# A table that sets the order of the engines' queues ahead of the FFN

## The chip, the cores and the metric

The kernel runs on one core of one Trainium2 chip. The metric is the device time of one execution in microseconds (us). A core has a matrix engine (PE, TensorE), a vector engine (DVE), a scalar engine for activations (ACT), a small general engine (POOL) and a queue that issues transfers (SP). Each of them works through its own queue of instructions in the order of that queue, and waits at an instruction until what it needs from the others is there. PE writes its results to PSUM, eight banks of 512 floats per partition; ACT and DVE read them from there.

## The reference

The reference is one block of a decoder, on 512 tokens of width 1024, all in float32:

```python
h = rmsnorm(x, norm1_g) * (1.0 + scale1) + shift1        # scale, shift, gate: c_act @ w_ada + b_ada
proj = h @ w_in                                          # x_rnn 1280, q_lat 384, kv_lat 256, k_rope 32, g_rnn, g_mla 1024 each
xc = causal_dwconv(x_rnn, conv_w, conv_b)                # width 4
y_rnn = rg_lru(xc, positions, ...)                       # two gates, a = exp(..), h[t] = a[t] * h[t-1] + b[t]
q = rmsnorm(q_lat) @ w_uq; kv = rmsnorm(kv_lat) @ w_ukv  # 16 heads, rotary on 32 of 96 columns
y_mla = causal_block_attention(q, k, v)
merged = sigmoid(g_rnn) * (y_rnn @ w_proj_rnn) + sigmoid(g_mla) * (y_mla @ w_proj_mla)
x = x + gate1 * (merged @ w_out)
h2 = rmsnorm(x, norm2_g) * (1.0 + scale2) + shift2
u = causal_dwconv(h2 @ w_up, ffn_conv_w, ffn_conv_b)     # 2 x 2816 columns, width 3
x = x + gate2 * ((silu(u_gate) * u_val) @ w_down)
return rmsnorm(x, final_g)
```

## The kernel before

**Tiles.** Columns of the weights lie on 128 partitions, the 512 tokens on the free axis, so one matmul is 128 x 128 weights by 512 tokens. For precision every operand is kept in two parts, a high one and the rest: `split` (L132, L133) copies the high part on ACT and subtracts it on DVE. A product then takes three matmuls (`mm3`, L164 to L166): high by high, high by low, low by high. Weights come by SP into one of three load buffers, `raw` (512 KB each), and are split from there into tiles `whl` and `whg`, two of each; one such tile is a *unit* of 512 columns, four blocks of 128, which twelve matmuls use. `Stream.get` (L153 issues its load) does this for the weights of all projections.

**PSUM.** The eight banks are shared out by tag: three `tr`, one `fil`, one `gm`, three `acc`. A new user of a bank waits until ACT or DVE has read the old one's result.

**Stages.** (1) *Start*: the modulation vectors of the first norm (DVE), the norm itself, transposes and the product with the latent columns. (2) *Attention*: 16 heads. `head_a` makes the scores, their maxima on DVE and the exponentials on ACT (L643), and transposes the result; `head_b` multiplies by the values. Between them stand the products for the next group of heads (`q_nope`, `k_nope`, `v_group`, all in bank `fil`) and 32 *fills*: halves of the products for the two merging gates, mostly in bank `gm`. Each second fill ends with a tanh that empties the bank (L466 ACT). `sums_rows` turns the sums of the softmax (L817) and spreads their inverses over the partitions with eight loads on POOL's queue (the spread loads, L823); `y_split` multiplies by them (L828). (3) *Recurrence*: `rnn_tile` for ten tiles of 128 channels: a product (bank `tr`), the convolution on DVE (L784), two gates (bank `acc`), tanh and exp on ACT (L792 to L797), a square root (L801), a scan on DVE (L805) and a last split into `yr`. Products of the attention's output, `pm_tile` 0 to 7, fill PE between the tiles. (4) *Projections*: eight products of the recurrence's result (called projection 0 to 7 here), each over ten chunks, chunk k being tile k; then the output product `wo` and, for each of four token blocks, the residual (L880, L881), the square (L913), the second norm (L915), transposes (L920), scale and shift (L925, L927) and a split (L929, L930). (5) *FFN*: 44 products with convolution, gating, and 22 chunks of the last product.

**What sets the order.** The code writes the operations in the order of its loops. A planner then puts each engine's instructions in a queue of their own: it goes through the program with estimated durations and takes, of what could run, what has the highest priority. The code steers it with `tc.high_priority(offset=...)`, with constants like `AHR` or `LOW` as offsets, and with `tc.issue_after(...)`, which fixes that one instruction stands behind another. PE's queue of before therefore mixes products where two had the same rank: the matmuls of fills 0 and 2 alternate one by one, and so do those of projections 2 and 3. Which buffer of a tag a tile gets also follows from that order.

Of the kernel before, what the change touches and what calls it, by code (L numbers as in the profile page):

```python
# [91 lines left out]

@with_exitstack
def block_kernel(ctx, tc, a):
    nc = tc.nc
# [670 lines left out]
    def tok(t):  # L766
        return slice(t * P, (t + 1) * P)

    with phase("p_rnn") as p2:
# [40 lines left out]
        def sums_rows():  # L810

            V.reciprocal(sums, sums)
            b = bank("tr")
# [3 lines left out]
            S.activation(rt[:HEADS, :], b[:HEADS, :], AF.Copy)  # L817
# [83 lines left out]
        h2 = st(sb, "A", 1, [P, NK, 2, T], F32R)  # L901
        for t in range(4):
            b = bank("fil" if t % 2 else "gm")
            for k in range(NK):
# [8 lines left out]
            S.activation(f[:, :T], x1[t][:, T:], AF.Square, accum_out=ssq)  # L913
# [1 line left out]
            V.tensor_scalar(f, x1[t], r[:, 0:1], -0.5, MUL, MUL)  # L915
            for i in range(2):
                b = bank("tr", (P, 4, P))
                for q in range(4):
                    k = 4 * i + q
                    PE.transpose(b[:, q, :], f[:, k * P:(k + 1) * P], ident)  # L920
# [8 lines left out]
                S.activation(dh, hi, AF.Copy)  # L929
# [208 lines left out]
```

## Time and profile before

| | |
|---|---|
| median of three runs | 888.75 us (887.96 to 891.56) |
| the profiled execution | 887.65 us |
| its span, from the first to the last instruction | 885.8 us |
| PE, matmuls | 859.3 us busy, 4030 instructions |
| PE, loading weights (runs beside the matmuls) | 688.8 us, 4030 |
| DVE | 643.3 us, 1212 |
| ACT | 491.1 us, 898 |
| POOL | 18.7 us, 43 |
| HBM read | 103.59 MB |

The profile gives, for each instruction, its line, the tile that it writes and those that it reads, its start and its duration, and what ended the idle time of its engine before it. `tr<-A,whl` is a product of activations `A` with weights `whl` into a bank of tag `tr`. A table of stretches gives, for each stretch of time, the busy time of each engine in it, the number of instructions in brackets, the clock granted to PE as a share of full speed, and the mean share of time in which the sixteen DMA engines were busy.

### The profile page before, as it was taken

Reading aid. Unit: us, or ns where it says so; the run is one execution under the profiler, and the core shown is the slowest. Engines: PE = TensorE matmul, PEld = TensorE weight load, DVE = VectorE, ACT = ScalarE, POOL = GpSimd, SP = SyncE. Lnnn points to the kernel's source line nnn. Section 1 sums busy time; section 2 is a strip of 40 time slices with the busy share of each in tenths; the row PEclk is TensorE's granted clock in tenths of the full one; section 3 lists DMA queues with packets and bytes.
Section 4 is the critical chain, followed back from the end, with each engine's and each line's share of the span. In section 5 each row is a group of like instructions: output and inputs, shape, how many; then the busy total and the mean of one; then the engine's idle time right before and its main releaser. Section 6 shows DMA issues by size and latency. Waiting matters only on the chain.

```text
span 885.8 us, 11220 instructions
## 1 busy us (share of the span) xinstructions
PE 859.3 (97%) x4030; PEld 688.8 (78%) x4030; DVE 643.3 (73%) x1212; ACT 491.1 (55%) x898; POOL 18.7 (2%) x43
## 2 busy tenths in 40 slices
PE   7999999999999999999999999999999999999996
PEld 4777878788767777777878898888788888888885
DVE  7978887989866899998555879766666666423524
ACT  7575777667645888887333554444544444322323
POOL 0001000001020000000000000000000000000000
PEclk9999999999999999999999999999999999999999
DMA  9824233344462243354325074332233333333322
GB/s 347 342 66 113 73 99 116 78 143 138 143 168 95 101 160 120 122 195 156 100 76 161 22 261 142 100 95 95 85 93 93 92 94 92 95 96 95 96 72 95
DMA packets 33804, 109.08 MB, mean 123 GB/s; under 512 B 4290, under 2 KB 8002, under 8 KB 33748
## 3 DMA queue, kind: packets, MB, share of 16 engines
q1 hardware_dynamic: 32116, 103.60, 35.7%
q0 software_dynamic: 1632, 4.75, 2.3%
q8 instruction: 32, 0.52, 0.2%
q14 instruction: 24, 0.20, 0.1%
HBM read 103.59 MB, written 2.13 MB: 119 GB/s over the span
## 4 chain that ended last, share of the span: by engine, by line
PE 63%; ACT 3%; DVE 3%; DMA 2%; issue 1%; POOL 0%; ACTq 0%; POOLq 0%; DVEq 0%
PE acc L164 9%; PE acc L166 9%; PE acc L165 9%; PE tr L164 4%; PE tr L166 4%; PE tr L165 4%; PE acc L762 2%; PE acc L764 2%; PE acc L763 2%; PE tr L1004 2%; PE tr L1006 2%; PE tr L1005 2%; PE gm L164 1%; PE gm L166 1%; PE gm L165 1%; PE fil L762 1%
## 5 line engine op out<-in xcount | busy, mean ns | idle before, releaser
L133 DVE TENSOR_TENSOR whg<-raw,whg 128x512 fp32r<-128x512 f32 x119 | 81.5, 688 | 82.1 <-ACT whg L132 81.8
L132 ACT ACTIVATE whl<-raw 128x512 fp32r<-128x512 f32 (+2 forms) x131 | 74.9, 577 | 112.4 <-PE acc L166 26.5
L132 ACT ACTIVATE whg<-raw 128x512 fp32r<-128x512 f32 x119 | 74.2, 627 | 103.3 <-PE acc L166 53.9
L133 DVE TENSOR_TENSOR whl<-raw,whl 128x512 fp32r<-128x512 f32 (+2 forms) x131 | 80.8, 622 | 52.9 <-ACT whl L132 52.3
L166 PE MATMUL acc<-A,whg 128*128 128x512 f32 x176 | 70.1, 398 | 0.1
L164 PE MATMUL acc<-A,whg 128*128 128x512 f32 x176 | 69.9, 397 | 0.3 <-ACT whg L132 0.2
L165 PE MATMUL acc<-A,whg 128*128 128x512 f32 x176 | 69.5, 395 | 0.0
L958 DVE SCALAR_TENSOR_TENSOR Y<-acc,vec,Y 128x511 f32<-128x511 f32 x86 | 64.3, 748 | 1.3
L166 PE MATMUL acc<-A,whl 128*128 128x512 f32 x160 | 63.2, 395 | 0.0
L165 PE MATMUL acc<-A,whl 128*128 128x512 f32 x160 | 63.2, 395 | 0.0
L164 PE MATMUL acc<-A,whl 128*128 128x512 f32 x160 | 63.1, 395 | 0.0
L643 ACT ACTIVATE P<-P,mx,qsc 128x512 f32<-128x512 f32 (+1 forms) x64 | 41.2, 647 | 7.1 <-DVE mx L639 7.0
L164 PEld LDWEIGHTS acc<-A,whg 128*128 128x128 f32 x176 | 33.0, 187 | 9.4 <-ACT whg L132 1.4
L166 PEld LDWEIGHTS acc<-A,whg 128*128 128x128 f32 x176 | 33.0, 187 | 8.9 <-DVE whg L133 0.7
L165 PEld LDWEIGHTS acc<-A,whg 128*128 128x128 f32 x176 | 33.0, 188 | 7.6
L164 PE MATMUL gm<-A,whg 128*128 128x512 f32 x88 | 35.7, 405 | 1.7 <-ACT R L466 1.2
L165 PEld LDWEIGHTS acc<-A,whl 128*128 128x128 f32 x160 | 30.0, 188 | 7.3
L956 ACT ACTIVATE Y<-acc,vec 128x512 f32<-128x512 f32 x43 | 32.9, 764 | 5.1 <-PE acc L166 5.1
L166 PEld LDWEIGHTS acc<-A,whl 128*128 128x128 f32 x160 | 30.0, 188 | 7.1
L164 PEld LDWEIGHTS acc<-A,whl 128*128 128x128 f32 x160 | 30.0, 188 | 7.1
L166 PE MATMUL gm<-A,whg 128*128 128x512 f32 x88 | 35.4, 403 | 0.0
L165 PE MATMUL gm<-A,whg 128*128 128x512 f32 x88 | 35.0, 398 | 0.0
(509 smaller groups left out, 2276.1 us busy)
## 6 DMA issues: line engine op xcount, KB each, us to landing
raw<-in_w_up SPq DMA_DIRECT2D x44, 512.0 KB, 3.5
raw<-in_w_dn SPq DMA_DIRECT2D x22, 512.0 KB, 3.6
wa<-in_w_adat SPq DMA_DIRECT2D x16, 512.0 KB, 9.7
raw<-in_w_adat SPq DMA_DIRECT2D x16, 512.0 KB, 3.3
raw<-in_w_xr SPq DMA_DIRECT2D x10, 512.0 KB, 4.1
raw<-in_w_pr SPq DMA_DIRECT2D x10, 512.0 KB, 3.8
raw<-in_w_gm SPq DMA_DIRECT2D x8, 512.0 KB, 3.6
raw<-in_w_gr SPq DMA_DIRECT2D x8, 512.0 KB, 3.5
```

Of the source, the lines that this page charges most:

```text
L132: S.activation(h, src, AF.Copy)
L133: return V.tensor_tensor(dst[:, 1, lo_c:lo_c + n], src, h.bitcast(F32), SUB).ins
L164: PE.matmul(out, wh, x[:, 0, xs], start=start, stop=False)
L165: PE.matmul(out, wh, x[:, 1, xs], start=False, stop=False)
L166: return PE.matmul(out, wl, x[:, 0, xs], start=False, stop=stop).ins
L643: S.activation(pq, pq, AF.Exp, scale=qsc[:, qb:qb + 1], bias=mx[:, qb:qb + 1], accum_out=sm[:, qb:qb + 1])
L762: PE.matmul(out, lt[:, 0, s], w[:, 0, :], start=start, stop=False)
L763: PE.matmul(out, lt[:, 0, s], w[:, 1, :], start=False, stop=False)
L764: return PE.matmul(out, lt[:, 1, s], w[:, 0, :], start=False, stop=stop).ins
L956: S.activation(u, b, AF.Identity, scale=vc("fw", 2 * 2 * NF + cj), bias=vc("fb", cj))
L958: V.scalar_tensor_tensor(u[:, d:], b[:, :T - d], vc("fw", (2 - d) * 2 * NF + cj), u[:, d:], MUL, ADD)
L1004: PE.matmul(b, lt[:, 0, s], w[:, 0, o:o + n], start=start, stop=False)
```

## The change

A table, `QUEUES`, holds one row for each of the five queues. `queue_order()` runs once, right before the FFN's code. It collects the instructions written so far, engine by engine, in the order in which the code wrote them, numbers them from 0 in base 36, and reads the engine's row: `9` is one entry, `b-c` a run of entries. Between each two neighbours of the row it adds a dependency of the kind NoSync, an order within one queue without a semaphore. The planner still runs; up to the FFN it has no choice of order left within a queue. No operation, tile or load is added or taken away. In ACT's row the first 25 entries, which hold the first norm's, are in the order that they had before.

The diff, with the table cut to the rows that are spoken of:

```diff
+QUEUES = {
+    "PE": """
+        0-8 b-c 9 d a e-u w-x 1h-1i v 10 13 y 1j 16 19 1c z 1k 11 14 12 15 22-25 17-18 1a-1b 1d-1g 1l 1o 1m 2n-2q 1n
...
+        r2-r3 wa wd wj-wk we-wi wb-wc wl vs-vz ry-s9 ty-u9 w0-w5 wm-wn w6 wo-wp v4 wq-wt w7-w9 v5-v7 wu-wv v8-v9
...
+        111 11e-11p zk-zp 11w-11x zq-zs 11y-127 zt-zz 128-129 100-103 11q 11t 12a-12c 11u 11r-11s 11v 12d-12j
+        12q-12t 13e-13f 12u-12v 13g-13p 12w-12z 13q-13r 130-136 13s-141 12k-12p 137-13d 148-14h 14w-14x 14i-14n
...
+        1bw-1bx 1cg-1cp 1by-1c1 1cq-1cr 1c2-1c5 1cs-1d1 1c6-1cd 1bk-1bm 1d8-1d9 1bn-1bp 1da-1dh 1d2 1d5 1di-1dl 1d6
+        1d3-1d4 1d7 1dw 1dm-1dv 1dx-1ej 1eq-1et 1fk-1fl 1eu 1fm-1fv 1ek-1ep 1ev-1ez 1fw-1fx 1f0 1ge-1gf 1fy-1gd
+        1gg-1ip 1f1 1iq 1f2 1ir 1f3 1is 1f4 1it 1f5 1iu 1f6 1iv 1f7-1fj 1iw-1jq 1kk-1kl 1jr-1kb 1kx 1kc-1kd 1ky
...
+    "DVE": """
+        0-3 a 4 b 5-9 c-k o l-m p-q n u-w s r t 10-12 y x z 16 14 17-18 13 15 1c-1d 1a 1e 19 1b 1i 1g 1j 1f 1h 1o 1u
...
+        ak-al an-ao c9 cb ap ca cc-cd cf aq ce cg-ch ar cj ci cl cn ck as cm co bu at bv c0 bw cp bx au by-bz cq c2
...
+        jz jt jy k0-k5 kc-kd k7-ka k6 kb ke-ki kp-kq kk-kn kr-kv kj ko kx-l0 kw l1""",
+    "Activation": """
+        0-3 6-7 4 8 5 9-n p o q s r t v-w u x-y 11 z-10 12 17-18 13-15 1g-1p 1w 16 1u 1q 1v 1r 1a 1y 8h-8i 19 1b
...
+        77 72 6w 73 7a 78 7b 7i-7k 7n-7q 7c 6n 7r-7s 7l 7v 7m 7w-7y 7d 7t 83 7z-80 7u 81 8j 82 85 84 86 88 8x-8y 87
+        89 8z-90 8b 91-92 8a 8c 93-94 8k-8l 8e 8o 8m 95 8d 8f 8n 96 8p 99 8q-8r 8t 8s 9i 97 8u-8v 9j 98 8w 9v-9w 8g
...
+        c6-c7 c9 cv c8 ck-cl cw cm-co cy ca cz cp cb d1 cq cc cr d2-d3 cx d5-d6 d8-da dc-dd df-dh dj d0 d4 dk d7 db
+        de dm-do di dq-dr dl ds-dt dp du-dv e2-e3 dw-dx e4-e9 dy-e1 ea-en eq eo-ep er-es ey et ez eu-ex f0-f5""",
+    "Pool": """
+        0 2 1 3-g i h j m l k n 11 p-q o r-10""",
+    "SP": """
+        0 2-a c b d-t 1 u-z 1b 10-1a 1c-25 2p 26-2o 2q-3g 3p-3q 3h-3k 3r-3s 3l-3o 3t-41""",
+}
...
+    def queue_order():
+        queues = {}
+        for ins in nc.cur_bb.bb.instructions:
+            if type(ins).__name__ not in ("BassTilePoolBoundary", "InstRegisterMove"):
+                queues.setdefault(str(ins.engine).split(".")[-1], []).append(ins)
+        for name, table in QUEUES.items():
+            order = []
+            for run in table.split():
+                ends = [int(v, 36) for v in run.split("-")]
+                order += queues[name][ends[0]:ends[-1] + 1]
+            for before, after in zip(order, order[1:]):
+                tc.add_manual_dep(after, before.name, mybir.DependencyInfo(
+                    mybir.DependencyClass.NoSync, mybir.DependencyReason.DATA), reason="order")
+
+    queue_order()
```

Some entries, to follow the table by: on PE, fill 21 is ty to u9 and fill 22 is v4 to vf; projection 0 is 1dw to 1ep (its last chunk 1en to 1ep), projection 1 is 1eq to 1fj, projection 5 is 1i2 to 1iv. On DVE, au splits the weights of fill 31, he is the last split of tile 9, kp and kq are L880 and L881 of the last token block. On ACT, 7d is the tanh of fill 21, 8f copies the weights of fill 31, ca and cp are the square roots of tiles 8 and 9, ey is the square (L913) of the last token block.

More of the change, by code (lines that the diff above doesn't have):

```diff
@@ L90 @@
 EARLY = 4
+QUEUES = {
+    "PE": """
+        0-8 b-c 9 d a e-u w-x 1h-1i v 10 13 y 1j 16 19 1c z 1k 11 14 12 15 22-25 17-18 1a-1b 1d-1g 1l 1o 1m 2n-2q 1n
+        1p-21 26-27 29 38-3b 28 2a-2m 2r 3t-3w 2s-37 3c-3s 3x 40 43 46 49 3y-3z 41-42 44-45 47-48 4a-4b 4e-4g 4c-4d
+        4h-4w 5j-5k 4x-5i 5l 7s-7t 5m-5r 7j-7q 7u-80 5s-66 7r 67-68 81-82 69-6v 83-89 6w-78 8m-8r 79-7c 91 94 9a 7d
+        92-93 9b 95-99 9c ba 8s-90 bb-bd bj-bk be-bi bl 7e-7h 9d-9h 9l 9i-9k 9m 7i 9n-9y 8a-8h 9z-ab bm-bp ac-ae
+        bq-bt 8i af-ao bu bw-bz cp cs cy bv 8j-8l c0 ct-cx c1-c3 cq-cr ap-ax cz-d0 ea ed-ei eb-ec ay-b1 ej-el b2
+        c4-cc b3-b9 dj-do cd-cl d1-d5 d9 d6-d8 da cm-co dy dp-dr db-dc em-et dd-di ds-dt eu-ev du-dx fg fj fp-fq
+        fk-fo fh-fi fr ew dz ex hp-hr e0 g2-gd hs-hx ey e1 ez e2 f0 e3 f1 e4 f2 e5 fs-fz f3 e6 ge-gp g0 gq-gt g1
+        e7-e9 gy-h3 gu-gx hy-hz j4 j7 i0 f4 j8-jc j5-j6 f5 jd-jf h4-hc f6-f7 i1-i5 i9 i6-i8 ia f8-fd ib-id ij-ir
+        jg-jj ie-ii fe-ff jk-jn kp ks ky-kz kt jo-jp ku-kx kq-kr l0 jq jy-jz jr-ju k0 hd k1 he k2 hf k3 hg-hi jv-jx
+        hj-hm lj-ll hn-ho lm-lt k4-k5 ng-ni k6-kc l1 l5-l9 l2-l4 la nj-nr lb-lf lu m5-mg lg-li is-ix mh-ms iy-j1 lv
+        lz m3 m0-m2 lw-ly n1-n6 m4 j2-j3 kd mt-mx p7-pa my-n0 pb-pf ke-kf n7-nf ns-nw o0 nx-nz o1 kg-km o2-o6 kn pg
+        ko o7-o9 ph-pi r4 r7-rc r5-r6 oa-oi rd-rf oj-om q1-q6 pj pn-pr pk-pm ps on-ow pt ox pu-px q7-qa py-q0 qb-qf
+        oy-p6 rg-rn sa sd-si sb-sc sj-sk sw ro-rp sl ua-ui rq-rx sx-t7 uj-ul qg-qj sm sq-st sn-sp t8-tb su-sv tc-tj
+        qk-qt tk-tm ts-tu tn-to tv-tx tp-tr um uq-ut vg vj vp un-up vh-vi vk-vo uu-uv vq-vr qu-qv uw-v0 qw-r1 v1-v3
+        r2-r3 wa wd wj-wk we-wi wb-wc wl vs-vz ry-s9 ty-u9 w0-w5 wm-wn w6 wo-wp v4 wq-wt w7-w9 v5-v7 wu-wv v8-v9
+        ww-wx 104-107 wy-x3 va-vf x4-z4 108-109 z5-z8 10a-10v z9-zf 112-113 zg-zh 114-11d zi 10w 10z zj 110 10x-10y
+        111 11e-11p zk-zp 11w-11x zq-zs 11y-127 zt-zz 128-129 100-103 11q 11t 12a-12c 11u 11r-11s 11v 12d-12j
+        12q-12t 13e-13f 12u-12v 13g-13p 12w-12z 13q-13r 130-136 13s-141 12k-12p 137-13d 148-14h 14w-14x 14i-14n
+        14y-157 142-147 158-159 14o-14s 15a-15j 14t-14v 15q-15v 16e-16f 15w-15x 16g-16p 15y-163 16q-16r 164-165
+        16s-16z 15k 170-171 15n 166-167 15l-15m 15o-15p 168-16d 178-17v 172 175 17w 173-174 176-177 17x-18h 18q-18r
+        18i-18j 18s-18y 19e-19f 18z-190 19g-19p 18k 18n 191-193 18l-18m 18o-18p 194 19q-19r 195 19s-1a1 196-19d
+        1a8-1a9 1aw-1ax 1aa-1aj 1ay-1b7 1ak-1an 1a2 1a5 1b8-1b9 1ao 1a3-1a4 1a6 1ba-1bj 1a7 1ap-1av 1bq-1bv 1ce-1cf
+        1bw-1bx 1cg-1cp 1by-1c1 1cq-1cr 1c2-1c5 1cs-1d1 1c6-1cd 1bk-1bm 1d8-1d9 1bn-1bp 1da-1dh 1d2 1d5 1di-1dl 1d6
+        1d3-1d4 1d7 1dw 1dm-1dv 1dx-1ej 1eq-1et 1fk-1fl 1eu 1fm-1fv 1ek-1ep 1ev-1ez 1fw-1fx 1f0 1ge-1gf 1fy-1gd
+        1gg-1ip 1f1 1iq 1f2 1ir 1f3 1is 1f4 1it 1f5 1iu 1f6 1iv 1f7-1fj 1iw-1jq 1kk-1kl 1jr-1kb 1kx 1kc-1kd 1ky
+        1ke-1kg 1ko 1kh 1kp 1ki 1kq 1kj 1l0-1l2 1kr 1ku-1kw 1l6-1l8 1ks-1kt 1kz 1l9-1la 1l3-1l4 1li 1lc 1l5 1lb
+        1ll-1lm 1lj-1lk 1lu-1lw 1ld-1le 1km-1kn 1lo-1lq 1lf-1lh 1ln 1lx-1ly 1m6-1m8 1mi-1mk 1m0 1mu 1m1-1m2 1lr
+        1mv-1mw 1ls-1lt 1lz 1m9-1ma 1mc-1md 1n6 1me 1m3 1n7-1n8 1m4-1m5 1mb 1ml-1mm 1mo-1mq 1mf-1mh 1mn 1mx-1my
+        1n0-1n2 1mr-1mt 1mz 1n9-1na 1n3-1n5 1nb 1o8-1oc 1nc-1nz 1od-1ou 1o0-1o7 1ov 1p4-1pr 1q0-1q2 1ow-1p3 1q3-1qn
+        1ps 1pw-1py 1pt-1pv 1pz 1qo-1qv""",
+    "DVE": """
+        0-3 a 4 b 5-9 c-k o l-m p-q n u-w s r t 10-12 y x z 16 14 17-18 13 15 1c-1d 1a 1e 19 1b 1i 1g 1j 1f 1h 1o 1u
+        1p 1v-1w 1k 1q 1x 1l 1y bs br 1z 1m 20 1s 21 1r 22 1t 1n 23 27-28 24-26 2d-2e 2g 2f 2i 2h 33-35 39 36-37
+        2j-2m 38 2n-2p 29 2v-2y 3a-3c 2a 2z 31 3d 30 32 3e 2b 3f 2q av ax 2r aw 2s ay 2t-2u az-b1 2c b2-b5 3g 3j
+        b6-b8 3h b9-bb 3i 3m bc-bf 3k 3x bg-bh 3p 3l bi 3q-3s bj 3t bk-bq 49 3n 4a-4c 3o 3y 3u 4d 3v 48 3w 3z 42 40
+        45 4e-4f 4p 41 43 4i 4g 44 4o 4r 4h 4s-4t 4q 46 4u 50 47 4v 58-5c 4j-4k 53 4l 57 56 4m 51 4n 52 4w-4y 5h 5q
+        5d-5e 4z 5f 54 5r 5j 5i 55 5k-5l 63 5m 64-65 5s 5n-5o 5g 5v 5t 5y 5p 61 5w 5u 66 5x 67 6k-6n 6c 6o 62 5z 68
+        60 69-6a 6j 6t 6d-6f 6b 6g 6q 6p 6h-6i 71-74 6r 6w 6u 75 70 6s 6v 7b-7d 6z 7a 7j 6x 7v 76-77 6y 7k 78 7e
+        7w-7y 7f 7l 79 7z 7u 7m 7o 7r 7g-7h 7p 7i 8f 7q 8a 8g-8h 84 7n 8c 7s 80-81 7t 8d 82 8e 8o 8i 8b 83 8j 8x-8z
+        85-87 90 88 8r 8w 8p 8l 8k 8q 8u 8m 89 91 97 8s-8t 8v 92 99 98 9a 93-94 9b 9g 9c 9h 8n 9r-9u 9i 9v 95 9p 9l
+        9d 9j 9e 96 9f 9q 9m 9k a4 9n 9w-9x a5-a7 9y a8 a1 ae-af 9o ad ag a9-aa ah a2 9z-a0 a3 bt ab am ai-aj ac
+        ak-al an-ao c9 cb ap ca cc-cd cf aq ce cg-ch ar cj ci cl cn ck as cm co bu at bv c0 bw cp bx au by-bz cq c2
+        cv c1 dj c3 d4 c4 cr dk c5 cs c6 ct c7 d5 cu c8 dl-dm da cx do d6 cw d7 e3 cy d8 cz dp e4 d0 d9 d1-d2 dq du
+        d3 e5 dr dn dc e6 db e8 ds dd dt de en-eo df e9 dg dw ee dv dh ep e7 eq es di dx ea dy eb f7 et f8 ec dz-e0
+        ed e1 eu ey f9 e2 er ev eg fa fc ef ew eh ex ei fr-fs ej fb ek fd el fi ez em ft-fu f0 fe fw ff-fg f1 gb fh
+        gc f2 fx f3-f4 g2 fk f5 fj gd f6 fv ge fy gg fl fz fm g0 fn gv g1 gh fo gw fp g4 fq gi gm gx gf gy h0 gj g3
+        gk g5 gl g6 h1 hf g7 hg g8-g9 h2 h6 h3 gz hh h4 ga go hk h5 gn hi hl gp h8 h7 hm hj gq h9 hq ha gr hr hb gs
+        hv hc gt hd gu he hn-ho hw-hx hp i1 hy-hz i2 i6 i3 i7-i8 ic i9-ia id ih ie ii if ij hs in ht i4 hu i0 io i5
+        ib ig is ik-il it im iu-iv ip-ir iw-iz je-jf j0-j1 jg-jk j2 j8 j3 j9 jb j4-j5 jc j6 jl j7 ja jd jm-js ju-jx
+        jz jt jy k0-k5 kc-kd k7-ka k6 kb ke-ki kp-kq kk-kn kr-kv kj ko kx-l0 kw l1""",
+    "Activation": """
+        0-3 6-7 4 8 5 9-n p o q s r t v-w u x-y 11 z-10 12 17-18 13-15 1g-1p 1w 16 1u 1q 1v 1r 1a 1y 8h-8i 19 1b
+        1s-1t 1x 1d 1c 1e 1z 22 20-21 25 23 2f 24 28-29 26 2a-2b 27 2g 2c-2d 1f 2q 2e 2h 2s-2v 2k 2i 2n 2w-2x 33 2j
+        2l 30 2y 2m 32 2z 2o 3c 2p 34-36 3k 3f 3l-3m 2r 3i 3n 3d 37 31 3e 38-39 3s 3a 40 3o-3p 3b 3q 3g 41 3h 3t-3w
+        42 3x-3y 3r 45 43 48 3z 3j 4b 46 44 47 4l 4d-4g 49 4o 4h 4a 4i-4j 4p 4w 4q-4s 4k 4n 4t 4z 4u 4m 4x 4v 4y
+        54-55 4c 52 56-57 5j 50 58-59 51 5a 5k-5l 5b-5f 5m 5o 5r 5u 5g-5h 5p 5i 5v-5w 5q 64 5x 62 5n 5s 5y-60 5t 6f
+        53 65 61 67-6a 6i 6g 63 6b-6d 6h 6l 6o-6p 6j 6q-6r 6k 6m 6s-6t 74 66 6e 6u 75 6x-6z 76 70 6v 7e-7g 79 7h 71
+        77 72 6w 73 7a 78 7b 7i-7k 7n-7q 7c 6n 7r-7s 7l 7v 7m 7w-7y 7d 7t 83 7z-80 7u 81 8j 82 85 84 86 88 8x-8y 87
+        89 8z-90 8b 91-92 8a 8c 93-94 8k-8l 8e 8o 8m 95 8d 8f 8n 96 8p 99 8q-8r 8t 8s 9i 97 8u-8v 9j 98 8w 9v-9w 8g
+        9m 9a 9x 9k 9b-9c 9e 9d 9y 9f 9l 9g 9z a1 9h aa 9n ab-ac 9o-9p 9r 9q a0 9s ad a2 ag a3 9t a4 ap a5 aq-ar 9u
+        a6 ae a7 as af a8 at av b4 a9 ah b5-b6 ai-aj al ak au am aw b7 an ba ax ao bj-bk b8 bl ay-b0 b9 b1 bm bb bp
+        b2 bc by bn b3 c0 bz bd-bg bo c1 bh bq bi c2 c4 cd br ce-cf bs bu bt c3 cg bv-bw ch cj bx cs-ct c5 cu ci
+        c6-c7 c9 cv c8 ck-cl cw cm-co cy ca cz cp cb d1 cq cc cr d2-d3 cx d5-d6 d8-da dc-dd df-dh dj d0 d4 dk d7 db
[5 more added lines that the diff above has]
+}
```

## The prediction

> **What bounds the kernel now.** I read the page's head first, then one table of stretches cut where the kernel's stages change, then the waits of TensorE (PE), then the timeline at the places where a wait ends. The head gives the whole:
>
> ```profile
> span 885.8 us, 11220 instructions
> ...
> PE 859.3 (97%) x4030; PEld 688.8 (78%) x4030; DVE 643.3 (73%) x1212; ACT 491.1 (55%) x898; POOL 18.7 (2%) x43
> ```
>
> PE is busy 97% of the span: 885.8 - 859.3 = 26.5 us idle. The table of stretches (length, then busy time and instructions of PE, weight loads PEld, DVE, ACT, POOL; clock; DMA share; GB/s) says where:
>
> ```profile
> 0.00:52.00 52.00, 46.96 (x182) 32.02 (x182) 44.19 (x98) 32.55 (x50) 1.70 (x12) 0.97 0.79 304
> 52.00:246.00 194.00, 187.65 (x1008) 153.66 (x1009) 166.31 (x421) 137.48 (x316) 10.88 (x21) 1.00 0.36 110
> 246.00:270.00 24.00, 22.34 (x97) 16.68 (x96) 15.26 (x25) 11.86 (x22) 5.20 (x9) 1.00 0.63 160
> 270.00:290.00 20.00, 19.24 (x83) 14.66 (x82) 12.13 (x20) 11.01 (x18) 0.00 (x0) 1.00 0.23 79
> 290.00:416.00 126.00, 122.65 (x516) 94.25 (x515) 116.73 (x180) 106.18 (x158) 0.00 (x0) 1.00 0.43 146
> 416.00:500.00 84.00, 83.45 (x367) 66.73 (x367) 51.44 (x92) 32.12 (x64) 0.00 (x0) 1.00 0.30 94
> 500.00:520.00 20.00, 18.48 (x135) 16.89 (x134) 16.45 (x38) 14.01 (x32) 0.95 (x1) 1.00 0.50 153
> 600.00:700.00 100.00, 100.00 (x431) 80.35 (x430) 69.06 (x100) 46.13 (x74) 0.00 (x0) 1.00 0.31 95
> 800.00:886.00 86.00, 78.57 (x404) 66.44 (x402) 35.97 (x72) 26.28 (x52) 0.00 (x0) 0.97 0.26 86
> ```
>
> Two blocks of idle are out of the table's reach or nearly: 52 - 46.96 = 5.0 us at the start, and 86 - 78.57 = 7.4 us at the end, behind the FFN. What a new order can touch is 6.35 (52 to 246, attention) + 1.66 + 0.76 + 3.35 (290 to 416, the recurrence) + 0.55 + 1.52 = 14.2 us.
>
> That is idle time alone. In the FFN (600 to 700) PE runs 431 matmuls in 100 us, 0.232 us each, with no idle: this is its full pace. At that pace the 516 matmuls from 290 to 416 would take 119.7 us, so 6.3 us are lost there where only 3.35 show as idle. The rest is the slow restart around each wait, which the records hide because one of them is longer (0.47 us in the row quoted further down) than its share of the pace. I take lost time as 1.9 times idle (6.3 / 3.35).
>
> **Which waits.** The waits of PE that lie past the start (what waited, for whom: us in total, times, longest):
>
> ```profile
> PE gm L164 <- ACT R L466: 1.9, 2, 1.2
> PE fil L611 <- DVE q L575: 1.6, 2, 1.3
> PE tr L164 <- ACT whl L132: 1.4, 3, 0.8
> PE tr L166 <- DVE whl L133: 1.0, 1, 1.0
> ...
> PE gm L166 <- DVE whg L133: 0.9, 1, 0.9
> ...
> PE tr L920 <- DVE R L915: 0.7, 1, 0.7
> ...
> PE acc L164 <- ACT A L929: 0.7, 1, 0.7
> ```
>
> None of these is a lack of work on ACT (55% busy) or DVE (73%). Each is an instruction that stood in its engine's queue behind another one, or a PSUM bank that PE wanted again at once.
>
> **The change part by part.** No operation is added, removed or resized: 2264 matmuls, 758 DVE, 546 ACT, 38 POOL and 145 SP instructions of the part up to the FFN get a fixed place. An entry is the instruction's number, in base 36, on its engine in the order in which the code writes them. The table's last SP run ends at 41 (number 145), one past the queue's last, 40, and a slice that ends too far takes nothing more. I followed the numbers through the code and set the table against the order in the trace.
>
> *Loads (SP, POOL).* Both rows are the order of before but for some swaps of neighbours. Cost 0; what moves is when their buffers come free.
>
> *Start, 0 to 52.* ACT's first 25 entries are as before. On DVE the two copies of the broadcast conditioning (a, b) now stand among the first norm's small operations instead of behind them. ACT, which reads that result, is still occupied with its squares then, and with DMA at 0.79 share the stretch waits for its loads. I take 0, between -0.5 and +0.5 us.
>
> *Attention and fills, 52 to 270.* Here is the largest wait, with what ACT did meanwhile:
>
> ```profile
> 247.59 0.59 ACT L817 ACTIVATE yr<-tr 16x512 f32<-16x512 f32 x1
> 248.09 0.57 ACT L466 ACTIVATE R<-gm 128x512 f32<-128x512 f32 x1
> ```
>
> ```profile
> 247.03 0.47 PE L166 MATMUL gm<-A,whg 128*128 128x512 f32 x1
> 248.71 0.51 PE L164 MATMUL gm<-A,whg 128*128 128x512 f32 x1 [1.21 <-ACT R L466]
> ```
>
> One bank serves the fills: fill 22 may start only when the tanh of fill 21 has read it, and that tanh (entry 7d) stood behind a copy for the softmax sums. PE lost 248.71 - 247.03 - 0.23 = 1.45 us. In the table 7d stands ahead of 7t, so ahead of these copies, and eleven other matmuls (w0-w5 wm-wn w6 wo-wp, about 1.3 us by their columns at the full pace) stand between the last of fill 21 (u9) and the first of fill 22 (v4). The same is done for the second such wait (1.9 - 1.2 = 0.7 us): sixteen matmuls, 16 x 0.232 = 3.7 us, now part the bank's old user from its new one. These two waits should go; what hides them is PE's own other work. At y_split, whose multiplications wait for the spread loads, one more weight split (ao) stands ahead of the waiting DVE instruction.
>
> The other attention waits I can't follow one by one. Some distances shrink: between the scores of head 5 and its transposes 4.8 us of matmuls (by columns at the full pace) stand where 8.6 stood, so new waits will come. All lost time here is 1.9 x (6.35 + 1.66) = 15.2 us, the most that can be won. The other bound is a loss of 2 us, if the waits move and the tight places add one like that at 247 and a half. I take 7, a little under half: DVE is busy 166.31 of 194 us here, so there is slack to use, but 86% leaves queues that jam.
>
> *Recurrence, 270 to 416.* This stage is bound by DVE more than by PE: 116.73 of 126 us. Two edits bear on it. First, the last fill's weight split (au on DVE, 8f on ACT) comes about 16 places earlier; it frees a load buffer, for which these stood waiting:
>
> ```profile
> 282.47 0.33 SPq L153 DMA_DIRECT2D raw<-in_w_xr  x1
> ...
> 286.79 0.63 ACT L132 ACTIVATE whl<-raw 128x512 fp32r<-128x512 f32 x1 [0.83 <-DMA raw<-in_w_xr]
> ...
> 287.48 0.50 PE L164 MATMUL tr<-A,whl 128*128 128x512 f32 x1 [0.76 <-ACT whl L132]
> ```
>
> Second, tiles 8 and 9 share one square-root stretch on ACT: ck-cl, cm-co (tile 9's tanh and exp) come ahead of ca, cp (both square roots). Each switch of function set costs a load:
>
> ```profile
> L801 ACT ACT_TABLE_LOAD x10 | 12.8, 1283 | 0.2
> L792 ACT ACT_TABLE_LOAD x8 | 10.3, 1283 | 0.1
> ```
>
> Two of these go, 2.6 us of ACT next to the end of the chain. DVE's idle time is 7.87 (270 to 290) + 9.27 (290 to 416) = 17.1 us; more than that the chain of ten tiles can't be shortened, and part of it is the chain's own latency. I take 7, between 0 and 14.
>
> *The price.* Tile 9's result gates the rest:
>
> ```profile
> 415.18 0.69 DVE L133 TENSOR_TENSOR yr<-pr,yr 128x512 fp32r<-128x512 f32 x1
> ...
> 416.01 0.43 PE L165 MATMUL tr<-yr,whl 128*128 128x512 f32 x1
> ```
>
> The matmul at 416.01 (1eo, projection 0, last chunk) starts when DVE has split tile 9. Before, 1864 PE instructions of this part stood ahead of it; in the table 1841 do, mostly because 19 matmuls of projection 1 (1f1 to 1fj), which filled this place, are put behind projection 4. PE will thus ask for tile 9 after 23 matmuls fewer: 23 x 0.232 = 5.3 us. PE's remaining work behind the gate is longer by as much. So the gate must open 5.3 us sooner only to break even: +5.3, a fixed term.
>
> *Projections to the second norm, 416 to 520.* Projection 1's late matmuls hold one whg and one whl weight tile, so projections 2 to 5 stream through one tile of each kind instead of two. A unit of weights is 12 matmuls, 2.8 us, and its two halves take about 0.6 us (ACT) and 0.7 us (DVE), with DVE busy 51.44 of 84 us: cover enough, I take +0.3, and up to 5 if half a microsecond is lost on each of ten units. At the end, the last token block waited for this:
>
> ```profile
> 504.47 0.69 DVE L880 TENSOR_TENSOR T<-fil,acc 128x512 f32<-128x512 f32 x1
> ...
> 511.17 0.69 DVE L881 TENSOR_TENSOR T<-T,Y 128x512 f32<-128x512 f32 x1
> ...
> 511.89 0.63 ACT L913 ACTIVATE R<-T 128x512 f32<-128x512 f32 x1 [0.48 <-DVE T L881]
> ```
>
> Between L880 and L881 lay 6 us of other DVE work. The table puts L881 (kq) right behind L880 (kp), and ACT's ey ahead of et; the two PE waits on L915 and L929 (0.7 each, 1.4) should go. I take -1.3, between 0 and 1.9 x 1.52 = 2.9.
>
> **Sum.** 0 - 7 - 7 + 5.3 + 0.3 - 1.3 = -9.7 us against the profiled execution, whose own time is 887.65 (span 885.8 and 1.85 around it): 878.0. The median of the runs is 888.75, 1.1 above it, so 879.
>
> [...]
>
> **The rivals.** *Waits only move (886.7).* For it: DVE at 86% in attention and 93% in the recurrence, in-order queues, and tighter places in the table. Against: the places I could follow are each cleared by what stood in the way. Half the gain of each stage: -3.5 - 3.5 + 5.3 + 0.3 - 0.7 = -2.1 from 887.65, then + 1.1, gives 886.7.
>
> *Slower: the gate at tile 9 (894).* Place: 1eo. If the chain of ten tiles, paced by DVE and by its loads, ends at 415.9 as now, everything PE won before stands still in front of it, and 5.3 us more work lie behind: 888.75 + 5.3 = 894. It decides where DVE's last split of tile 9 comes less than about 1 us earlier; from 1 to 5.3 us it is a draw. Against it: the chain starts only when attention is over, so what is won there moves its start too.
>
> *Far faster (869).* PE restarts cost as much as the idle time, so clearing a wait pays twice: 15.2 x 0.8 in attention, 12 of DVE's idle in the recurrence, 2.5 at the end: -12.2 - 12 + 5.3 - 2.5 = -21.4, 867 to 869. Against it: it needs 93%-busy DVE to become nearly gapless.
>
> **How the numbers follow.** The forecast, 879, has its own range 873 to 885 and a chance of 0.51. Waits only move: 0.21. Gate: 0.13. Far faster: 0.15. A measurement of this kernel can tell about 0.5%, 4.4 us, from no change: faster is under 884.3, slower over 893.2. Faster: 0.51 less 0.03 of its upper edge, 0.15, and 0.02 of the second case: 0.65. Slower: the gate, 0.13. The rest, 0.22. The range reaches from 867.5 to 891: the gate and a little below are left out, under 0.2.
>
> **What would show it.** Right: no PE wait on L466; the 1.28 us table loads number 25 instead of 27; the last split of tile 9 near 402 and projection 0's last chunk just behind it; PE idle from 52 to 270 near 4; no 0.7 us waits on L915 and L929. Wrong: PE idle for microseconds just ahead of projection 0's last matmuls (the gate); new waits on the weight splits of projections 2 to 5; waits in attention as long in sum as now under other names.

## The result, and the profile after

The changed kernel takes 878.94 us (878.41 to 880.0, four runs) against 888.45 (887.96 to 891.56) of the kernel before: a ratio of 0.9887, 95% interval 0.9863 to 0.9912, 9.5 us less. Forecast were 879.0, and 9.7 less. The profiled execution took 880.0, that of before 887.65; the sections below say why these two differ by 7.65 only. One execution of rec (2971.41 us) and the profiled one of gateloads (2919.74) took over three times as long as all others; the ratios leave them out, and the two medians hold them and would be 0.13 us or less lower without.

The head of the page of the changed kernel, and its table of stretches (columns as before). The table in the kernel adds 72 lines, so L466 is now L538, L132 and L133 are L204 and L205, L915 is L987; lines behind `queue_order()` stand 94 later (L1006 is L1100). In most kernels of the experiments lines stand one or two lower, by the length of their tables.

```profile
span 878.2 us, 11212 instructions
...
PE 858.8 (98%) x4030; PEld 688.6 (78%) x4030; DVE 640.6 (73%) x1212; ACT 488.1 (56%) x896; POOL 18.7 (2%) x43
```

```profile
0.00:52.00 52.00, 46.80 (x178) 32.27 (x179) 44.52 (x100) 32.70 (x50) 1.70 (x12) 0.93 0.77 296
52.00:246.00 194.00, 191.44 (x1038) 157.23 (x1037) 166.42 (x421) 140.39 (x319) 11.33 (x22) 1.00 0.36 116
246.00:270.00 24.00, 22.99 (x95) 17.14 (x94) 15.83 (x26) 11.53 (x21) 4.70 (x8) 1.00 0.65 174
290.00:416.00 126.00, 124.48 (x519) 94.57 (x518) 117.43 (x184) 102.56 (x156) 0.00 (x0) 1.00 0.44 145
500.00:520.00 20.00, 20.00 (x173) 20.00 (x172) 18.32 (x37) 11.77 (x25) 0.17 (x1) 1.00 0.82 282
```

PE's idle time from 52 to 270 us fell from 8.0 us to 2.56 + 1.01 = 3.6, from 290 to 416 from 3.35 to 1.52, from 500 to 520 from 1.52 to nothing. Over the whole span it fell from 26.5 to 878.2 - 858.8 = 19.4 us: 7.1 of the 7.6 us by which the span is shorter are idle time of PE that is gone. Its waits past the start that are 0.3 us or longer in sum are now these:

```profile
PE tr L236 <- ACT whl L204: 1.3, 2, 1.0
PE acc L703 <- DMA q<-rp: 0.8, 1, 0.8
PE tr L725 <- DVE Y L743: 0.7, 1, 0.7
PE tr L238 <- DVE whl L205: 0.6, 1, 0.6
PE tr L237 <- DVE yr L205: 0.5, 1, 0.5
PE fil L236 <- DVE spc L823: 0.4, 1, 0.4
PE tr L992 <- DVE R L987: 0.3, 1, 0.3
PE gm L834 <- DVE T L952: 0.3, 1, 0.3
```

No wait on the tanh (L538) is left, and that was the largest sum of before past the start, 1.9 us. The tanh of fill 21 (7d) runs as soon as its bank is full:

```profile
238.69 0.60 ACT L538 ACTIVATE R<-gm 128x512 f32<-128x512 f32 x1 [0.16 <-PE gm L238]
```

**Where the time went.** I cut both traces at places that are the same work: the last matmul of the latent columns, the last split of the attention's output (ysplit), tile 9's last split, the last product of the first half of `wo`, and PE's last matmul. Before (tile 9's row, 415.18, stands in the prediction), then after:

```profile
51.29 0.63 PE L406 MATMUL tr<-A,wls 128*64 128x512 f32 x2
268.20 1.29 DVE L133 TENSOR_TENSOR yhl<-Y,yhl 128x512 fp32r<-128x512 f32 x2
479.87 0.39 PE L764 MATMUL gm<-whg,yhl 128*128 128x512 f32 x1
878.29 0.28 PE L1006 MATMUL acc<-A,ff 128*128 128x256 f32 x1
```

```profile
52.63 0.62 PE L478 MATMUL tr<-A,wls 128*64 128x512 f32 x2
264.24 1.28 DVE L205 TENSOR_TENSOR yhl<-Y,yhl 128x512 fp32r<-128x512 f32 x2
403.84 0.69 DVE L205 TENSOR_TENSOR yr<-pr,yr 128x512 fp32r<-128x512 f32 x1
473.10 0.39 PE L836 MATMUL gm<-whg,yhl 128*128 128x512 f32 x1
870.16 0.28 PE L1100 MATMUL acc<-A,ff 128*128 128x256 f32 x1
```

From the ends of these rows, and of the same rows in the traces of the experiments (us; the last column leaves the start out):

| kernel | latents end | attention: to ysplit | chain: ysplit to tile 9 | tile 9 to `wo` half | to PE's end | sum behind the latents |
|---|---|---|---|---|---|---|
| before | 51.9 | 217.6 | 146.4 | 64.4 | 398.3 | 826.6 |
| after | 53.3 | 212.3 | 139.0 | 69.0 | 396.9 | 817.2 |
| att | 52.3 | 211.2 | 148.1 | 64.4 | 397.8 | 821.5 |
| rec | 52.3 | 217.1 | 140.9 | 69.0 | 396.5 | 823.5 |
| stall | 51.6 | 214.0 | 139.3 | 69.0 | 396.5 | 818.9 |
| start | 53.1 | 212.6 | 139.4 | 69.0 | 396.6 | 817.7 |
| fill31 | 52.3 | 211.5 | 145.2 | 69.0 | 396.5 | 822.2 |
| loads2 | 53.6 | 211.9 | 142.9 | 69.3 | 396.6 | 820.7 |
| pair | 51.7 | 211.9 | 142.9 | 69.0 | 396.5 | 820.3 |
| gate | 51.9 | 211.7 | 139.2 | 70.9 | 396.5 | 818.3 |
| gate5 | 52.1 | 212.2 | 139.9 | 69.1 | 396.5 | 817.7 |
| gateloads2 | 53.1 | 212.2 | 142.0 | 73.9 | 396.6 | 824.7 |
| tail | 52.1 | 211.5 | 140.2 | 69.0 | 396.5 | 817.2 |

Attention -5.3, chain -7.4, behind the chain +4.6, output and FFN -1.4: -9.5 in all. Against the -9.5 stands +1.3 at the start of this one execution. Chain and what follows it have to be read together, -2.8: PE is busy nearly all the time, so work that it no longer does ahead of tile 9 it does behind it. Eight of the traces have the changed kernel's order up to ysplit, and their second column goes from 211.5 to 212.3 (att, 211.2, nearly so); in the last column after and tail agree, at 817.2, and start lies 0.5 above. So differences under 0.8 us in the one and 0.5 in the other say nothing.

### The profile page after: what moved, and what is told of

Same layout as the page of the kernel before. It is cut to its first block, busy times and chain, and to the rows that moved or that the text cites. A ratio compares the mean times of both kernels' runs of the same rounds, so it can differ in the third digit from the quotient of the medians.

```text
span 878.2 us, 11212 instructions
## 1 busy us (share of the span) xinstructions
PE 858.8 (98%) x4030; PEld 688.6 (78%) x4030; DVE 640.6 (73%) x1212; ACT 488.1 (56%) x896; POOL 18.7 (2%) x43
## 4 chain that ended last, share of the span: by engine, by line
PE 72%; DVE 10%; ACT 8%; DMA 7%; issue 3%; POOL 0%; SPq 0%; DVEq 0%; ACTq 0%; POOLq 0%
PE acc L237 9%; PE acc L238 9%; PE acc L236 9%; PE tr L238 3%; PE tr L236 3%; PE tr L237 3%; PE acc L834 2%; PE acc L836 2%; PE acc L835 2%; DMA wa<-in_w_adat 2%; PE tr L738 2%; PE tr L1098 2%; PE tr L1100 2%; PE tr L1099 2%; PE gm L236 2%
## 5 line engine op out<-in xcount | busy, mean ns | idle before, releaser
L205 DVE TENSOR_TENSOR whg<-raw,whg 128x512 fp32r<-128x512 f32 x119 | 81.6, 688 | 86.8 <-ACT whg L204 86.5
L204 ACT ACTIVATE whl<-raw 128x512 fp32r<-128x512 f32 (+2 forms) x131 | 75.2, 576 | 110.8 <-PE acc L238 29.5
L204 ACT ACTIVATE whg<-raw 128x512 fp32r<-128x512 f32 x119 | 74.2, 627 | 98.5 <-PE acc L238 58.6
L205 DVE TENSOR_TENSOR whl<-raw,whl 128x512 fp32r<-128x512 f32 (+2 forms) x131 | 81.3, 621 | 56.2 <-ACT whl L204 55.9
L1052 DVE SCALAR_TENSOR_TENSOR Y<-acc,vec,Y 128x511 f32<-128x511 f32 x86 | 64.4, 749 | 1.3
L715 ACT ACTIVATE P<-P,mx,qsc 128x512 f32<-128x512 f32 (+3 forms) x64 | 41.2, 645 | 17.5 <-DVE mx L711 17.5
```

The source lines that it names most:

```text
L204: S.activation(h, src, AF.Copy)
L205: return V.tensor_tensor(dst[:, 1, lo_c:lo_c + n], src, h.bitcast(F32), SUB).ins
L715: S.activation(pq, pq, AF.Exp, scale=qsc[:, qb:qb + 1], bias=mx[:, qb:qb + 1], accum_out=sm[:, qb:qb + 1])
L1052: V.scalar_tensor_tensor(u[:, d:], b[:, :T - d], vc("fw", (2 - d) * 2 * NF + cj), u[:, d:], MUL, ADD)
```

## The experiments

**Two halves.** *att* takes the changed kernel's order for what starts ahead of 266 us in its trace, and the order of before for all the rest; *rec* the order of before up to 270 us, and the changed kernel's behind it. Each is written as a full table.

```diff
 # att: entries of the new table with a start under 266 us, then the remaining ones as before
-order = new
+order = [k for k in new if start_after[k] < 266] + [k for k in before if start_after[k] >= 266]
 # rec: the other way round, cut at 270 us of the trace of before
-order = new
+order = [k for k in before if start_before[k] < 270] + [k for k in new if start_before[k] >= 270]
```

> The order of the changed kernel up to the end of attention (266 us: 1275 PE, 441 DVE, 315 ACT instructions) and the order of before for everything behind it. Theory: PE lost 5.1 us less by 270 us in the changed kernel and the chain of tiles starts 4.0 us earlier; without the later order nothing is taken back, so 888.45 less 4 to 6.5: 882 to 884.5. The prediction's term alone would give 881.5. Rival (waits only move, or the gate swallows it): 886.5 to 888.5.

> The other half: the order of before up to 270 us (1269 PE, 440 DVE, 313 ACT instructions) and the order of the changed kernel behind it. Theory: the two halves add up; behind 270 us the changed kernel's PE lost about 3 us less (0.7 in the recurrence, 2.2 behind it), so 885 to 886. Prediction's terms: -7 + 5.3 + 0.3 - 1.3 = -2.7, 885.8. Rival, the gate: with the chain starting as late as before, tile 9 comes after PE has asked for it, 889 to 892.

Measured: att 883.29 (ratio 0.9947, 0.9931 to 0.9963), rec 885.37 (0.9971, 0.996 to 0.9981), against 887.99: -4.7 and -2.6. Neither half is swallowed. They add up to 7.3, not 9.5, which the intervals leave open; in the table they add up to 5.1 + 3.1 = 8.2 of 9.4. In att the chain takes 148.1 us instead of 146.4, so it seems that the old order of the recurrence gave back part of what attention had won.

**A wait in attention.** *stall* puts the tanh of fill 21 three entries back.

```diff
-7w-7y 7d 7t 83 7z-80
+7w-7y 7t 83 7z 7d 80
```

> The changed kernel, but the tanh of fill 21 (7d) stands three entries later on ACT, behind the copies 7t, 83 and 7z, so that it ends near 241.5 us instead of 239.3, while fill 22's first matmul (v4) asks for its bank at 240.0: one wait of about 1.45 us, as the largest one of before. It measures what such a wait costs. Theory (1.9 times, as taken in the prediction): plus 2.8, 881.7. Wait alone: 880.4. Rival: it is made up later, where the chain of tiles or a transfer sets the time, 878.9.

Measured: 879.96 (0.9908, 0.9889 to 0.9927), so 1 us above the changed kernel at an uncertainty as large. The trace tells more. PE has the same order in both kernels, so each matmul can be set against the same one. First the changed kernel, then *stall*, around fill 22's first matmul:

```profile
239.88 0.38 PE L725 MATMUL tr<-ident,P 128*128 128x128 f32 x2
240.02 0.48 PE L236 MATMUL gm<-A,whg 128*128 128x512 f32 x1
```

```profile
238.56 0.38 PE L724 MATMUL tr<-ident,P 128*128 128x128 f32 x2
240.12 0.50 PE L235 MATMUL gm<-A,whg 128*128 128x512 f32 x1 [1.18 <-ACT R L537]
```

Ahead of the wait *stall* runs 239.88 - 238.56 = 1.32 us earlier than the changed kernel (its start went better), behind it 0.10 later, and it is 0.12 later at ysplit as well (265.64 against 265.52). A wait of 1.18 us idle, nearly the 1.21 of before, thus costs 1.4 us, 1.2 times what it lasts and not 1.9 times, and none of it is made up by the end of attention.

**The start.** *start* has the order of before for all that starts ahead of 52 us.

> The order of before up to 52 us (175 PE, 81 DVE, 44 ACT instructions) and that of the changed kernel behind it. In the profiled executions the changed kernel stands 1.3 us behind at 52 us, with a clock of 0.50 from 15 to 20 us (before 0.72) and 0.92 from 20 to 25 us (before 1.00). Theory: this is the clock of that execution and not the order, 878.9 (878.3 to 879.5). Rival: the order of the start costs it, 877.6.

```diff
 # start: as rec, cut at 52 us
-order = new
+order = [k for k in before if start_before[k] < 52] + [k for k in new if start_before[k] >= 52]
```

Measured: 880.42 (0.9907, 0.9889 to 0.9924), no gain, and its latents end as late as in the changed kernel, at 53.1. The granted clock explains it. The stretch from 15 to 20 us, before, after, in *start* and in *gate*:

```profile
15.00:20.00 5.00, 4.51 (x16) 3.52 (x15) 5.00 (x11) 4.97 (x8) 0.00 (x0) 0.72 1.03 407
```

```profile
15.00:20.00 5.00, 4.60 (x11) 3.63 (x12) 5.00 (x11) 4.96 (x8) 0.00 (x0) 0.50 1.03 405
```

```profile
15.00:20.00 5.00, 4.74 (x11) 3.78 (x12) 5.00 (x11) 4.97 (x8) 0.00 (x0) 0.50 1.03 405
```

```profile
15.00:20.00 5.00, 4.39 (x19) 3.22 (x20) 5.00 (x11) 4.93 (x8) 0.00 (x0) 1.00 1.04 408
```

The changed kernel ran at half clock there (0.50), *gate*, with the same start, at full clock, and its latents end 1.4 us sooner. In the table the latents end at 53.1 or later in after, start, loads2 and gateloads2, the four traces with 0.50 in this stretch, and at 52.3 or sooner in all others, whichever order the start has. The start's 1.3 us are the execution's, not the order's.

**The early split of the last fill.** *fill31* has, from ysplit to about the first tile, 90 PE, 29 DVE and 27 ACT entries in the order of before. The core of it:

```diff
 ACT
-8m 95 8d 8f 8n 96 ... 97 8u-8v 9j 98 8w
+8m 95 8n 96 ... 97 9i 8u-8v 98 9j 8f 8d 8w
 DVE
-bw cp bx au by-bz ... d5 cu c8
+bw cp bx-bz ... d5 au cu c8
```

> The changed kernel, but the stretch from the end of attention to about the first tile (90 PE, 29 DVE, 27 ACT entries) stands as before: the last fill's weight split is back at place 332 on ACT (8f, instead of 319) and 463 on DVE (au, instead of 447), and its matmuls at 1362 to 1387 on PE (instead of 1348 to 1371). The prediction gave this early split and the load buffer that it frees a share of the 7 us: 881 to 883. Theory by the traces, where the chain up to tile 8 became only 1.0 us shorter: 879 to 880.

Measured: 883.99 (0.9958, 0.9946 to 0.997): 5.1 us slower than the changed kernel. My theory from the traces was wrong; the prediction's step points the right way. The chain takes 145.2 us, 6.1 more. The last fill's weights are copied at 286.31 instead of 273.75, and the loads behind it in SP's queue wait for buffers. The fourth of the ten loads of recurrent weights goes out at 293.69 instead of 290.61, and PE waits for these weights:

```profile
293.69 0.33 SPq L225 DMA_DIRECT2D raw<-in_w_xr  x1
...
297.20 0.63 ACT L204 ACTIVATE whl<-raw 128x512 fp32r<-128x512 f32 x1 [2.64 <-DMA raw<-in_w_xr]
```

```profile
PE tr L236 <- ACT whl L204: 4.8, 4, 2.6
```

```profile
298.00:300.00 2.00, 2.00 (x8) 1.64 (x9) 1.66 (x3) 0.45 (x1) 0.00 (x0) 0.85 0.39 156
300.00:302.00 2.00, 2.00 (x6) 1.54 (x6) 2.00 (x4) 0.00 (x0) 0.00 (x0) 0.50 0.00 0
302.00:304.00 2.00, 2.00 (x8) 1.47 (x7) 0.51 (x2) 0.99 (x2) 0.00 (x0) 0.80 0.00 0
```

Behind the wait of 2.6 us the clock fell to a half: 2 x 0.15 + 2 x 0.50 + 2 x 0.20 = 1.7 us more are lost. Also the second wait on the tanh of before came back (0.69 us, at 294.1 here and at 300.2 before). The edit restores the order of this whole stretch, so the 5.1 us are not the price of the one split alone.

**The shared square-root stretch.** *loads2* puts tile 8's square root ahead of tile 9's tanh and exp, which brings back two table loads; *pair* restores the order of before on ACT and DVE for the last parts of both tiles.

```diff
 loads2, ACT
-c8 ck-cl cw cm-co cy ca cz cp
+c8 ca ck-cl cw cm-co cy cz cp
 pair, ACT
-c6-c7 c9 cv c8 ck-cl cw cm-co cy ca cz cp cb d1 cq cc cr
+c6 cv c7 c9 c8 cw ca ck cz cy cb cl-cm cc cn-co d1 cp-cr
 pair, DVE
-gp h8 h7 hm hj gq h9 hq ha gr hr hb gs hv hc gt hd gu he
+gp hm gq-gs h8 hr hq gt h7 gu h9 hv ha-he hj
```

> The changed kernel, but tile 8's square root (ca) stands again ahead of tile 9's tanh and exp (ck to co) on ACT, so that two more function tables are loaded there (27 instead of 25, 2 x 1.28 = 2.6 us). Theory: ACT is busy without a gap from 386.4 to 399.9 us, tile 9 comes 2.6 us later, and PE, which already waits 0.53 us for it, waits longer: plus 2.6 us (wait alone) to 4.9 (1.9 times), 881.5 to 883.8. Rival: the loads lie beside other work and the end of tile 9 hardly moves, 878.9.

> The changed kernel, but the last two tiles of the recurrence are taken one behind the other again: on ACT the entries c6 to cr and on DVE gp to he stand among themselves as before (27 table loads instead of 25), PE's row is that of the changed kernel. In the traces tile 9 ends 0.8 us behind tile 8 in the changed kernel and 7.2 us behind it before, while tile 8 itself comes only 1.0 us sooner after the end of attention. Theory: the pairing is what shortened the chain; undone, tile 9 is 4 to 7 us later and PE waits at projection 0's last chunks: 883.5 to 886.5. Rival: only the two table loads count, 2.6 us, and the time is that of the kernel with them alone, 883.4. Other rival: PE's row has enough ahead of these chunks, 879 to 880.

Measured: loads2 883.37 (0.9942, 0.9929 to 0.9956), 4.4 us slower; pair 882.26 (0.9945, 0.9931 to 0.9959), 3.3 slower. The chain is 3.9 us longer in both, and *pair* has the two loads as well; beyond them the pairing shows no gain. The changed kernel has 9 + 7 such loads where 10 + 8 stood:

```profile
L873 ACT ACT_TABLE_LOAD x9 | 11.5, 1283 | 0.2
L864 ACT ACT_TABLE_LOAD x7 | 9.0, 1283 | 0.1
```

But PE's wait is not the one that I had named. In loads2 it stood still for a weight copy of projection 2 (d1), which stands behind the square root on ACT; ACT's row comes first, then PE's:

```profile
402.51 0.61 ACT L203 ACTIVATE whg<-raw 128x512 fp32r<-128x512 f32 x1
```

```profile
400.04 0.39 PE L235 MATMUL tr<-yz,whl 128*128 128x512 f32 x1
403.18 0.79 PE L235 MATMUL tr<-yz,whg 128*128 128x512 f32 x1 [2.76 <-ACT whg L203]
...
404.20 0.63 PE L236 MATMUL tr<-yz,whl 128*128 128x512 f32 x1
404.63 0.63 PE L237 MATMUL tr<-yz,whg 128*128 128x512 f32 x1
```

The matmuls behind it start 0.43 us apart, at full pace 0.232.

**The gate.** In the changed kernel PE does wait there, for the low half of tile 8 (1el), and not for tile 9, which comes 0.8 us behind it:

```profile
402.75 0.49 PE L236 MATMUL tr<-yr,whl 128*128 128x512 f32 x1
403.78 0.50 PE L237 MATMUL tr<-yr,whl 128*128 128x512 f32 x1 [0.53 <-DVE yr L205]
```

*gate* puts 22 matmuls of projection 1 ahead of it again, *gate5* five, *gateloads* 22 and the table loads of loads2.

```diff
 PE, gate
-1eu 1fm-1fv 1ek-1ep 1ev-1ez 1fw-1fx 1f0 ... 1iv 1f7-1fj
+1eu 1fm-1fv 1ev-1fd 1ek-1em 1fe-1fg 1en-1ep 1fh-1fj 1fw-1fx
 PE, gate5
-1fm-1fv 1ek-1ep 1ev-1ez
+1fm-1fv 1ev-1ez 1ek-1ep
 gateloads: gate on PE and loads2 on ACT
```

> The changed kernel, but 22 matmuls of projection 1 (1ev to 1fg) stand again ahead of 1eo, the first matmul that needs tile 9, so that 1863 PE instructions of this part are ahead of it (before 1864, changed kernel 1841). Theory: the chain of ten tiles ends at its own time, and the 5.3 us were never a price that is paid by themselves; PE waits 0.53 us for tile 9 in the changed kernel, that wait goes, worth 0.5 to 1.0 us: 877.9 to 878.4 against 878.9. Rival, the fixed term of the prediction: the 5.3 us come back, 873.6. Other rival: the queue of PE jams on the weights of projection 1, 880 or more.

> The changed kernel, but five matmuls of projection 1 (1ev to 1ez, 1.16 us) stand ahead of projection 0's last two chunks, where PE waited 0.53 us for the low half of tile 8. Theory: the wait goes and nothing behind it moves, 877.9 to 878.4. Rival: it only moves to the gate row's weights, as with 22 matmuls, 879 to 880.3.

> Both edits at once: the 22 matmuls ahead of tile 9 and the two more table loads. Theory: PE now has 5.1 us of work more before it asks for tile 9, which covers the 2.6 us, so the time is that of the first edit alone, 877.9 to 878.6. Rival: two table loads cost 2.6 us wherever they stand, about 881.

Measured: gate 880.28 (0.9911, 0.9897 to 0.9924), 1.3 us above the changed kernel; gate5 879.04 (0.9904, 0.989 to 0.9919), the same as it; gateloads 886.56 (0.9984, 0.9974 to 0.9994). The wait of 0.53 went in the first two and the time did not. In gate5 PE waits 0.72 us for a weight copy at 405.8 in its place. In gate, PE used projection 1 up sooner and then stood still for the operand of the gate row, a modulation vector that a product with ones spreads over the partitions (L561):

```profile
442.24 0.49 PE L561 MATMUL tr<-whl,ones 128*128 128x512 f32 x1 [1.01 <-ACT whl L203]
443.46 0.50 PE L561 MATMUL tr<-whl,ones 128*128 128x512 f32 x1 [0.72 <-DVE whl L204]
```

gateloads missed its theory by 8 us, so I took it once more, for a trace, as *gateloads2*:

> The kernel with both edits (22 matmuls ahead, two table loads more) once more, for an undisturbed trace, since its 886.6 us was 6 to 8 us above what the theory gave. Theory: ACT comes later with everything behind the square roots, above all the weight copies of the projections, while PE now uses up projection 1 sooner, so that PE waits for weights and not for tile 9: waits of 5 us or more in sum on weight copies between 405 and 445 us. Rival: PE waits for tile 8 or 9. Other rival: the clock, 0.990 to 0.993 in those executions against 0.995, and then the lost time is spread over the whole and the time is nearer to 880.

Measured: 886.01 (0.9987, 0.9975 to 0.9999). Its trace has both kinds of wait:

```profile
PE tr L235 <- ACT whg L203: 2.7, 1, 2.7
PE tr L561 <- ACT whl L203: 1.0, 1, 1.0
PE tr L561 <- DVE whl L204: 0.7, 1, 0.7
```

They are 2.7 us for the weight copy d1, which the 22 matmuls can't cover because it lies ahead of projection 2 and not at tile 9, and 1.0 and 0.7 for the gate row. And behind both the clock fell; here is the second time, and the same stretch of gate, which had the same two waits at full clock:

```profile
450.00:455.00 5.00, 5.00 (x17) 3.92 (x16) 1.94 (x3) 1.54 (x3) 0.00 (x0) 0.66 0.01 2
```

```profile
450.00:455.00 5.00, 5.00 (x23) 4.04 (x22) 2.07 (x3) 0.63 (x1) 0.00 (x0) 1.00 0.36 105
```

5 x 0.34 = 1.7 us again. The sum 2.7 + 1.7 + 1.7 + 1.7 = 7.8, less the 0.5 saved, is about the 7.5 that the table shows. So the expectation was right that the waits are on copies and splits of operands, but they are 4.4 us and not 5 or more, and its rival, the clock, had its share as well: 3.4 us, at two places and not spread over the whole.

**The last token block.** *tail* puts L881 and the square back behind the other block's scale and shift.

```diff
 ACT
-er-es ey et ez eu-ex
+er-ez
 DVE
-kp-kq kk-kn
+kp kk-kn kq
```

> The changed kernel, but the last token block's operations stand as before: L881 (kq) behind the scale and shift of the block ahead of it instead of right behind L880 (kp), and the square (ey) behind that block's scale and shift on ACT. Theory of the prediction: the last token block comes 1.3 us later, 880.2 (878.9 to 881.8). Rival: FFN products of PE's queue cover it and nothing moves, 878.9.

Measured: 879.53 (0.9903, 0.9889 to 0.9916), and 396.5 us from the `wo` half to the end, as all the others with the new order. Undoing this edit loses nothing, although other DVE work lies between L880 and L881 again (L951 and L952 here):

```profile
497.22 0.68 DVE L951 TENSOR_TENSOR T<-fil,acc 128x512 f32<-128x512 f32 x1
...
501.51 0.68 DVE L952 TENSOR_TENSOR T<-T,Y 128x512 f32<-128x512 f32 x1
```

## Why the prediction was right

The total was right to 0.1 us, the terms less so, and that they add up so well is partly luck: against the table attention won 1.7 us less than put down, and the other terms together 1.5 us more.

- *Start, 0.* Right. The +1.3 of the profiled execution is the clock, and *start* wins nothing.
- *Attention and fills, -7.* Right in kind, too large: -5.3 in the trace, -4.7 in att. The two waits on the tanh went (the second, at 300.2 us, lay in the recurrence and not in this term), and of the 1.6 us on L575 0.2 are left. Which of the other edits won what was not separated. The step that failed is "1.9 times idle". *stall* shows 1.2 times, and so did the prediction's own row: 1.45 us lost for 1.21 idle. The factor came from one stretch, 290 to 416, and doesn't hold there either: by the same sum the changed kernel loses 126 - 519 x 0.232 = 5.6 us for 1.52 idle, so 1.83 us of idle time less gave back only 0.7. The bounds of this term, 15.2 us above all, were therefore too wide, and with them the third rival.
- *Recurrence, -7.* Right: the chain is 7.4 us shorter. Both places named bear on it: undone, the stretch with the early split costs the chain 6.1 us and the two table loads 3.9. That is 10.0, more than the 7.4; but in both runs the clock fell behind a wait (2.6 us in fill31, 2.8 in loads2), for 1.7 us each, which the trace of before never shows in this stage (1.00). So these are prices in the new order and not shares of the 7.4; the shares stay open. Tile 9's last split begins at 403.84, not near 402; 1.3 us of that is the clock at the start.
- *The gate, +5.3, and the weight tiles, +0.3.* The size was nearly right: 4.6 us more from tile 9 to the `wo` half. But I called it a price, and it is only work that changed sides: *gate* put it back and won nothing. PE arrives at tile 8 half a microsecond early, so chain and work are balanced to that. With it the chain's 7.4 us are worth 2.8, where the prediction had 7 - 5.3 - 0.3 = 1.4. None of the feared waits on the weight splits of projections 2 to 5 came.
- *The last token block, -1.3.* The size was right (-1.4), the cause wrong: *tail* undoes the edit that I named and keeps the gain. The distance of L880 and L881 is 4.3 us there, 6.7 before. What else in the order behind the projections brings it was not separated, and neither was whether the FFN, whose order the planner still chooses, has a part in it.
- *Rivals.* "Waits only move" falls with att and rec, which each keep their gain; a small part of it may be true, in the 1.7 us that att's chain gives back. The slower case needed a chain that doesn't come sooner; it came 11.3 us sooner. The far faster one needed the factor of 1.9.
- *Against the median.* The profiled executions differ by 7.65 us, the medians by 9.5. Of the 1.85 between these, the clock at the start makes up 1.3.

## What to carry to other kernels

When an order is fixed by hand, follow what stands behind each late instruction in its own queue: both costly reversals here (a weight copy behind a square root, a load behind one whose buffer a late split held) hurt at places that the moved instruction has nothing to do with. Cut two traces at places that are the same work, and set each term of a forecast against its own stretch. Price a wait of PE of a microsecond or so at little more than what it lasts (1.4 us for 1.18 here); the four of 2.6 to 2.8 us cost an estimated 1.7 us more each, by the clock in the stretches behind them. Between 1.5 and 2.6 us the traces have none behind the start, so the price there was not shown.
